# Retention products in two fp32r parts: chunk states and masked scores with v

## Chip, cores and metric

The kernel runs on one core of one Trainium2 chip. The metric is the device time of one launch in microseconds; the median of three runs before the change is 1696.02 us (1693.71 to 1698.85).

## What is computed

A decoder trunk of two residual layers on 1024 positions with 1024 channels, in float32. The even layer has a combined input projection, an S5 state-space branch, a retention branch with four heads, and one output projection; the odd layer is a gated MLP. The change touches the retention branch alone:

```python
    scores = jnp.einsum('bcnhk,bcmhk->bchnm', qc, kc) * decay[None, None]
    inner = jnp.einsum('bchnm,bcmhv->bcnhv', scores, vc)
    local = jnp.einsum('bcmhk,bcmhv->bchkv', kc * zeta[None, None, :, :, None], vc)

    def step(state, s_chunk):
        return state * chunk_decay[None, :, None, None] + s_chunk, state
    ...
    cross = jnp.einsum('bcnhk,bchkv->bcnhv', qc * xi[None, None, :, :, None], prev)
    o = (inner + cross).reshape(bsz, seq, RET_HEADS, RET_DV)
```

Positions are cut into eight chunks of 128. Within a chunk the masked scores multiply v (`inner`); to that comes q times the state that the earlier chunks left (`cross`), and the state grows by k^T v of each chunk (`local`). A group norm per head follows, then a gain and a gate. In the kernel the state update is a plain sum, S + k^T v, and the mask a product with one 128x128 tile, `causal`.

## The kernel before

The work is one long program for one core. TensorE (PE) does the products, VectorE (DVE) and ScalarE (ACT) the elementwise work, GpSimd (POOL) some of it, and SyncE (SP) issues nearly all DMAs, in the order of its queue. Instructions on an engine run in the order in which the program has them; that order comes from a scheduler that sorts by data and buffers, so a change of tiles or buffers moves instructions.

Most products elsewhere take fp32 operands as two fp32r parts: `split` (line 63) casts to hi on ACT and subtracts on DVE to get lo, and `mm3` (line 99) makes three matmuls, hi x hi, hi x lo and lo x hi, summed in PSUM. Retention uses plain fp32 matmuls, each of which stands in the trace as two PE instructions.

`attend(h, nh, ...)` does half of a head's positions, four chunks. There are eight of them, (0,0), (0,1), (1,0) ... (3,1). Its parts: scores k q into `ps_s` (L1100); the mask on DVE, `sd` (L1102); `keys_by_token`, which transposes k into `ps_kt` (L1087) and copies it to `kz` on ACT (L1089); then for each chunk a state product `ps_st` from kz and v (L1112, two of them, and only for seven of a head's eight chunks), a cross product from q and S into `ps_o` (L1115, two), and the inner product from sd and v into the same `ps_o` (L1116); the new state S is the sum of `ps_st` and the old one on DVE (L1122). `ps_o` is copied to `on` by ACT (L1126) and normalised on DVE (L1130 to L1136).

`finish` of that attend is handed to the next one, which calls it between its own key transposes and products (`mid()`). For each of two halves d it loads the gate `bz` (L1143), transposes `on` into `ps_ot` (L1146), makes `yb` = ps_ot x gain x bz on DVE (L1148) and stores it to `yab_d` (L1149). `ps_s`, `ps_kt`, `ps_st` and `ps_ot` are all tiles of the PSUM pool `psE` with the tag "a", and rotate through its three buffers.

The S5 branch's gate, `glu(j)`, fills PE between the steps: `ps_gl` products, a sigmoid `sg` on ACT, products of sg with `yf` and with `az` on DVE (L1073, L1076), and a store of `az` to `yab_d` (L1077).

After the last attend comes the even output projection (`strassen_out`): it loads tiles of `yab_d` (`slB..`, L1226) and weights (`raw`, `wr`, L1238), forms sums of them on DVE (L1274, L1275, L1296, L1297), splits them (`yhi`, `ylo`, `whi`, `wlo`) and multiplies into `ps_acc`. Its tile `t2` (t in the rows, L1274) lies in memory that the retention pools had.

Of the kernel before, what the change touches and what calls it, by code (L numbers as in the profile page):

```python
# [9 lines left out]
F32 = mybir.dt.float32  # L10
F32R = mybir.dt.float32r
# [14 lines left out]
def tile_hybrid_trunk(ctx: ExitStack, tc: tile.TileContext, A, out, dbg=None):  # L26
    nc = tc.nc
    PS = bass.MemoryType.PSUM
    ld = nc.sync.dma_start
# [28 lines left out]
    vv_d = dd("vv_d", [8, 128, 1024])  # L58
# [4 lines left out]
    def split(hi, lo, src, E=nc.vector):  # L63
        nc.scalar.copy(hi, src)  # L64
        E.tensor_tensor(lo, src, hi.bitcast(F32), SUB)  # L65
# [33 lines left out]
    def mm3(ps, lh, ll, rh, rl, first, last, hold=None, chain=False):  # L99
        with tc.issue_after(hold.ins) if hold else ExitStack():  # L100
            nc.tensor.matmul(ps, lh, rh, start=first, stop=False, skip_group_check=chain)  # L101
        nc.tensor.matmul(ps, lh, rl, start=False, stop=False, skip_group_check=chain)  # L102
        return nc.tensor.matmul(ps, ll, rh, start=False, stop=last, skip_group_check=chain)  # L103
# [77 lines left out]
    for e in seqE:  # L181
# [5 lines left out]
        else:  # L187
            nm, h = seqB[e]
# [30 lines left out]
    hh, hl = zip(*[[hp.tile([128, 8, 512], F32R, tag=f"h{e}{t}", name=f"h{e}{t}") for e in "hl"] for t in range(2)])  # L219
# [51 lines left out]
    with tc.tile_pool(name="s5p", bufs=1, reuse_waits="tile") as pp:  # L271
# [234 lines left out]
        for o_, f in zip(ph, (cs, sn)):  # L506
            for k in range(2):
                sl = slice(64 * k, 64 * k + 64)
# [7 lines left out]
        for tabC, tabS, e0, n in ((C0, S0, 0, 16), (C1, S1, 4, 8)):  # L516
            V.memset(tabC[:, :, 0:1], 1.0)
            V.memset(tabS[:, :, 0:1], 0.0)
            m = 1
            while m < n:  # L520
# [4 lines left out]
                cl, sl = tabC[:, :, 0:m], tabS[:, :, 0:m]  # L525
                ch, sh = tabC[:, :, m:2 * m], tabS[:, :, m:2 * m]
# [154 lines left out]
    for n in range(16):  # L681
        b, h = n // 2, n % 2
# [156 lines left out]
    def raw_of(nm, h, t):  # L839
        g, b = {"q": ("q", 4), "k": ("k", 4), "v": ("a2", 2)}[nm]  # L840
        if nm == "v":
            r_ = rq.tile([128, 4, 256], F32, tag=g, name="vraw", bufs=b)
            ld(out=r_, in_=vv_d[4 * t:4 * t + 4, :, h * 256:(h + 1) * 256].rearrange("c p d -> p c d"))
        else:
            r_ = rq.tile([128, 2, 512], F32, tag=g, name=nm + "raw", bufs=b)
            ld(out=r_, in_=qk_d[nm, h][:, :, t * 512:(t + 1) * 512])
        return r_
# [67 lines left out]
    for n, e in enumerate(seqE):  # L915
# [8 lines left out]
        if e == "z":  # L924
            i = cnts["z"]
# [121 lines left out]
    rp = eb.enter_context(tc.tile_pool(name="ret", bufs=1, reuse_waits="tile"))  # L1047
    gy = ExitStack()
    gp = gy.enter_context(tc.tile_pool(name="glu", bufs=1, side="right", reuse_waits="tile"))
# [29 lines left out]
    def keys_by_token(kr, n):  # L1079
        kz = []  # L1080
        for i in range(n):
            if i % 2 == 0:
                m = min(2, n - i)
                pk = psE.tile([128, 2, 2, 128], F32, tag="a", name="ps_kt")
                for c in range(m):
                    for d in range(2):
                        nc.tensor.transpose(pk[:, c, d, :], kr[:, d, (i + c) * 128:(i + c + 1) * 128], ident)  # L1087
                kt = rp.tile([128, 2, 2, 128], F32, tag="kz", name="kz", bufs=3)
                nc.scalar.copy(kt[:, 0:m], pk[:, 0:m])  # L1089
            kz.append(kt[:, i % 2])  # L1090
        return kz

    lastmm = {}

    def attend(h, nh, q, k, v, S, mid=None):
        ps = psE.tile([128, 4, 128], F32, tag="a", name="ps_s")
        for i in range(4):
            c = slice(i * 128, (i + 1) * 128)
            for e in range(2):
                nc.tensor.matmul(ps[:, i, :], k[:, e, c], q[:, e, c], start=e == 0, stop=e == 1)  # L1100
        sd = rp.tile([128, 4, 128], F32, tag="sd", name="sd", bufs=2)
        nc.vector.tensor_tensor(sd, ps, causal.unsqueeze(1).to_broadcast([128, 4, 128]), MUL)  # L1102
        kz = keys_by_token(k, 3 if nh else 4)
        if mid:
            mid()
        po = psO.tile([128, 4, 256], F32, tag="o", name="ps_o")
        for i in range(4):
            c = slice(i * 128, (i + 1) * 128)
            if i < len(kz):
                pl = psE.tile([128, 2, 256], F32, tag="a", name="ps_st")  # L1110
                for d in range(2):
                    nc.tensor.matmul(pl[:, d, :], kz[i][:, d, :], v[:, i, :], start=True, stop=True)  # L1112
            if S is not None:
                for d in range(2):
                    nc.tensor.matmul(po[:, i, :], q[:, d, c], S[:, d, :], start=d == 0, stop=False)  # L1115
            lastmm[h, nh, i] = nc.tensor.matmul(po[:, i, :], sd[:, i, :], v[:, i, :], start=S is None, stop=True)  # L1116
            if i < len(kz):
                Sn = rp.tile([128, 2, 256], F32, tag="S", name="S", bufs=3)
                if S is None:
                    nc.scalar.copy(Sn, pl)  # L1120
                else:
                    nc.vector.tensor_tensor(Sn, pl, S, ADD)  # L1122
                S = Sn
        on = gp.tile([128, 4, 256], F32, tag="on", name="on")
        for e in range(2):
            nc.scalar.copy(on[:, 2 * e:2 * e + 2], po[:, 2 * e:2 * e + 2])  # L1126
        st = small.tile([128, 4, 6], F32, tag="bst", name="bst")
        mv = small.tile([128, 4, 2], F32, tag="bmv", name="bmv")
        for n in range(4):
            nc.vector.bn_stats(st[:, n, :], on[:, n, :])  # L1130
            nc.vector.bn_aggr(mv[:, n, :], st[:, n, :])
        va = small.tile([128, 4], F32, tag="bva", name="bva")
        nc.vector.tensor_scalar(va, mv[:, :, 1], EPS, None, op0=ADD)  # L1133
        r = rstd_of(va, 4)
        for n in range(4):
            nc.vector.tensor_scalar(on[:, n, :], on[:, n, :], mv[:, n, 0:1], r[:, n:n + 1], op0=SUB, op1=MUL)  # L1136
        return (lambda: finish(h, nh, on)), S

    def finish(h, nh, on):
        for d in range(2):  # L1140
            j = 2 * h + d
            bz = gp.tile([128, 512], F32, tag="bz", name="bz", bufs=2)
            ld(out=bz, in_=bz_d[j][:, nh * 512:(nh + 1) * 512])  # L1143
            pt = psE.tile([128, 4, 128], F32, tag="a", name="ps_ot")
            for n in range(4):
                nc.tensor.transpose(pt[:, n, :], on[:, n, d * 128:(d + 1) * 128], ident)  # L1146
            yb = gp.tile([128, 512], F32, tag="yb", name="yb", bufs=2)
            nc.vector.scalar_tensor_tensor(yb, pt.rearrange("p n c -> p (n c)"), cols[:, 8 + j:9 + j], bz, op0=MUL, op1=MUL)  # L1148
            ld(out=yab_d[8 + j][:, nh * 512:(nh + 1) * 512], in_=yb)  # L1149

# [8 lines left out]
    for n, (h, nh) in enumerate(steps):  # L1159
        o = pre[h, nh]  # L1160
        if nh == 0:
            S = None
        if nh == 0:
            pre[h, 1] = prefetch(h, 1)
        e1, S = attend(h, nh, o["q"], o["k"], o["v"], S, e1)
# [235 lines left out]
    gp = odd.enter_context(tc.tile_pool(name="sg", bufs=1, reuse_waits="tile"))  # L1401
# [20 lines left out]
    with tc.tile_pool(name="sv", bufs=2, reuse_waits="tile") as vp, tc.tile_pool(name="psV", bufs=3, space=PS, reuse_waits="tile") as psV, \  # L1422
# [10 lines left out]
        for th in range(2):  # L1433
            acc = [psVa.tile([128, 512], F32, tag="acc", name="ps_v2") for _ in range(4)]
            for u in range(4):
                wu = w_next()
                for kk in range(2):
                    k = 2 * u + kk
                    bh, bl = B[k // 4, th]
                    for i in range(4):  # L1440
                        sl = slice(i * 128, (i + 1) * 128)
# [9 lines left out]
            g = th + 1  # L1451
# [236 lines left out]
```

## Time and profile before

| | |
|---|---|
| runs, us | 1696.02 median (1693.71, 1696.02, 1698.85) |
| profiled execution, us | 1695.32 |
| span of its profile, us | 1693.6 |
| PE busy | 1598.4 us, 94% of the span |
| DVE busy | 1277.3 us, 75% |
| POOL busy | 745.8 us, 44% |
| ACT busy | 609.8 us, 36% |

The profile shows one execution. Times in its rows are microseconds from the start of the span. A busy share over the whole span is an average of stages with different limits, so the tables by stretches of the span say more. In a row of the timeline, [x <-Y] is idle time x of the engine just before the row and what ended it; matmuls overlap, so the time that one costs is read from start to start, and not from its own duration.

### The profile page before, as it was taken

The page shows a single profiled execution, that of the slowest core. Times are in us where ns is not written, and L with a number is a line of the kernel's source. Part 1 is how long each engine was busy: PE and PEld are TensorE (multiplying, and loading weights), DVE is VectorE, ACT ScalarE, POOL GpSimd, SP SyncE. Part 2 cuts the span into 40 slices and gives each one's busy share as a digit, 9 for nine tenths or more (in the row PEclk, how much of TensorE's full clock was granted, in tenths as well). Part 3 has the DMA queues.
Part 4 walks back from the last instruction along what each step waited for, and adds up shares of the span by engine and source line. Part 5 has one row for each costly group of instructions (what it writes and reads, how often), then busy time and mean ns, then how long its engine had stood idle before and what let it go on. Part 6 is the DMA issues. An engine that isn't in the chain of part 4 may idle for free.

```text
span 1693.6 us, 22715 instructions
## 1 busy us (share of the span) xinstructions
PE 1598.4 (94%) x8364; PEld 1351.2 (80%) x8364; DVE 1277.3 (75%) x1951; ACT 609.8 (36%) x787; POOL 745.8 (44%) x521
## 2 busy tenths in 40 slices
PE   7979999998999999999969999899999999989996
PEld 6757888875898977888758888898888888868775
DVE  7857766559778576565896879768988888858876
ACT  6413433432122222122223445332444444442344
POOL 4476876627654432000062544423454444425252
PEclk9989999997999999999989999999999999999998
DMA  8246776641555379654975443434333333388433
GB/s 222 63 124 145 169 184 150 167 128 55 174 181 173 112 265 297 226 192 140 318 276 177 144 155 113 139 106 130 96 103 100 100 100 100 100 291 268 161 125 112
DMA packets 260974, 270.18 MB, mean 160 GB/s; under 512 B 31968, under 2 KB 186368, under 8 KB 260864
## 3 DMA queue, kind: packets, MB, share of 16 engines
q1 hardware_dynamic: 255104, 256.15, 49.6%
q10 hardware_dynamic: 5760, 12.59, 2.0%
q8 instruction: 66, 1.08, 0.3%
q14 instruction: 44, 0.36, 0.1%
HBM read 195.28 MB, written 67.11 MB: 155 GB/s over the span
## 4 chain that ended last, share of the span: by engine, by line
PE 66%; DVE 13%; DMA 9%; issue 5%; POOL 4%; ACT 2%; SPq 1%; POOLq 0%; ACTq 0%; DVEq 0%
PE ps_uz L102 7%; PE ps_uz L103 7%; PE ps_uz L101 7%; PE ps_acc L102 3%; PE ps_vx L102 3%; PE ps_vx L103 3%; PE ps_vx L101 3%; PE ps_acc L101 3%; PE ps_acc L103 3%; DVE wlo L65 3%; PE ps_z L101 2%; PE ps_z L102 2%; PE ps_z L103 2%; PE ps_gl L102 2%; PE ps_gl L103 2%
## 5 line engine op out<-in xcount | busy, mean ns | idle before, releaser
L101 PE MATMUL ps_acc<-whi,yhi 128*128 128x512 f32 x448 | 177.3, 403 | 18.1 <-ACT yhi L64 7.0
L102 PE MATMUL ps_acc<-wlo,yhi 128*128 128x512 f32 x448 | 180.8, 404 | 13.7 <-DVE wlo L65 13.7
L64 ACT CAST whi<-raw 128x1024 fp32r<-128x1024 f32 x110 | 115.6, 1050 | 215.5 <-PE ps_uz L102 49.1
L103 PE MATMUL ps_acc<-whi,ylo 128*128 128x512 f32 x448 | 177.5, 400 | 0.0
L65 DVE TENSOR_TENSOR wlo<-raw,whi 128x1024 fp32r<-128x1024 f32 x94 | 132.2, 1406 | 32.9 <-ACT whi L64 32.1
L101 PEld LDWEIGHTS ps_acc<-whi,yhi 128*128 128x128 f32 x448 | 86.5, 194 | 40.1 <-ACT yhi L64 7.5
L1580 DVE TENSOR_SCALAR vy<-vy,mu,rs 128x128 f32<-128x128 f32 x128 | 113.4, 952 | 2.6 <-DMA vy<-v_d 2.3
L102 PEld LDWEIGHTS ps_acc<-wlo,yhi 128*128 128x128 f32 x448 | 86.8, 194 | 35.7 <-DVE wlo L65 16.4
L103 PEld LDWEIGHTS ps_acc<-whi,ylo 128*128 128x128 f32 x448 | 86.1, 192 | 19.3
L64 ACT CAST whi<-s 128x1024 fp32r<-128x1024 f32 x60 | 62.7, 1047 | 102.3 <-POOL s L724 35.2
L101 PE MATMUL ps_z<-hh,whi 128*128 128x512 f32 (+1 forms) x248 | 95.1, 386 | 0.8 <-ACT hh L64 0.8
L102 PE MATMUL ps_z<-hl,whi 128*128 128x512 f32 (+1 forms) x248 | 95.4, 385 | 0.5 <-DVE hl L65 0.5
L103 PE MATMUL ps_z<-hh,wlo 128*128 128x512 f32 (+1 forms) x248 | 94.0, 379 | 0.0
L65 DVE TENSOR_TENSOR wlo<-s,whi 128x1024 fp32r<-128x1024 f32 x60 | 79.2, 1321 | 16.1 <-ACT whi L64 16.1
L725 POOL TENSOR_TENSOR s<-raw 128x512 f32<-128x512 f32 x25 | 39.0, 1561 | 107.7 <-DMA raw<-in_w_in_odd 83.1
L112 POOL TENSOR_TENSOR rs_r<-bva,nhalf 128x4 f32<-128x4 f32 x8 | 8.5, 1057 | 165.9 <-DVE bva L1133 165.9
L723 POOL TENSOR_TENSOR s<-raw 128x512 f32<-128x512 f32 x25 | 33.7, 1348 | 67.5 <-DMA raw<-in_w_in_odd 28.8
L101 PE MATMUL ps_uz<-hh,whi 128*128 128x512 f32 x144 | 57.3, 398 | 1.1 <-ACT hh L64 0.9
L102 PE MATMUL ps_uz<-hl,whi 128*128 128x512 f32 x144 | 57.1, 396 | 0.0
L103 PE MATMUL ps_uz<-hh,wlo 128*128 128x512 f32 x144 | 56.7, 394 | 0.0
L65 POOL TENSOR_TENSOR wlo<-raw,whi 128x1024 fp32r<-128x1024 f32 x16 | 40.9, 2554 | 34.7 <-ACT whi L64 34.7
L65 DVE TENSOR_TENSOR whl<-raw,whl 128x512 fp32r<-128x512 f32 x25 | 30.4, 1215 | 31.2 <-ACT whl L64 31.2
(561 smaller groups left out, 5133.1 us busy)
## 6 DMA issues: line engine op xcount, KB each, us to landing
raw<-in_w_in_odd SPq DMA_DIRECT2D x50, 512.0 KB, 3.9
raw<-in_w_in_even SPq DMA_DIRECT2D x48, 512.0 KB, 4.2
raw<-in_w_out_even SPq DMA_DIRECT2D x28, 512.0 KB, 4.5
raw<-in_w_out_odd SPq DMA_DIRECT2D x28, 512.0 KB, 4.3
wr<-in_w_out_even SPq DMA_DIRECT2D x16, 512.0 KB, 6.0
vy<-v_d SPq DMA_DIRECT2D x32, 256.0 KB, 3.0
y_d<-c SPq DMA_DIRECT2D x32, 256.0 KB, 3.1
wr<-in_w_out_odd SPq DMA_DIRECT2D x16, 512.0 KB, 4.9
```

What stands on the lines that cost most here:

```text
L64: nc.scalar.copy(hi, src)
L65: E.tensor_tensor(lo, src, hi.bitcast(F32), SUB)
L101: nc.tensor.matmul(ps, lh, rh, start=first, stop=False, skip_group_check=chain)
L102: nc.tensor.matmul(ps, lh, rl, start=False, stop=False, skip_group_check=chain)
L103: return nc.tensor.matmul(ps, ll, rh, start=False, stop=last, skip_group_check=chain)
L112: nc.gpsimd.tensor_tensor(r, v, nhalf[:, 0:n], ALU.pow)
L723: P.tensor_tensor(s14[:, 0:4], a21, a22, ADD)
L725: P.tensor_tensor(s23[:, 4:8], a11, a21, SUB)
L1580: V.tensor_scalar(vy[:, c, :], vy[:, c, :], mu2[:, cc:cc + 1], rs2[:, cc:cc + 1], op0=SUB, op1=MUL)
```

## The change

The state products and the inner products take hi and lo parts of their operands and go through `mm3`: three fp32r matmuls in place of one plain one. For that v is split at the start of each attend (`vh` in a new tile, lo in place of the loaded v, which keeps the name `vraw`), the masked scores into `sh` and `sl`, and the transposed keys, as they leave PSUM, into `kzh` and `kzl`. Cross products and scores stay as they are. To make room, buffers are cut: `sd` 2 to 1, `S` 3 to 2, `bz` 2 to 1, `yb` 2 to 1; `kz` with three becomes two each of `kzh` and `kzl`.

```diff
-            r_ = rq.tile([128, 4, 256], F32, tag=g, name="vraw", bufs=b)
+            r_ = rq.tile([128, 4, 256], F32R, tag=g, name="vraw", bufs=b)
...
-                kt = rp.tile([128, 2, 2, 128], F32, tag="kz", name="kz", bufs=3)
-                nc.scalar.copy(kt[:, 0:m], pk[:, 0:m])
-            kz.append(kt[:, i % 2])
+                kt = [rp.tile([128, 2, 2, 128], F32R, tag="kz" + e, name="kz" + e, bufs=2) for e in "hl"]
+                split(kt[0][:, 0:m], kt[1][:, 0:m], pk[:, 0:m])
+            kz.append([x[:, i % 2] for x in kt])
...
     def attend(h, nh, q, k, v, S, mid=None):
+        vh, vl = rq.tile([128, 4, 256], F32R, tag="x", name="vh", bufs=2), v
+        split(vh, vl, vl.bitcast(F32))
...
-        sd = rp.tile([128, 4, 128], F32, tag="sd", name="sd", bufs=2)
+        sd = rp.tile([128, 4, 128], F32, tag="sd", name="sd")
         nc.vector.tensor_tensor(sd, ps, causal.unsqueeze(1).to_broadcast([128, 4, 128]), MUL)
+        sh, sl = [rp.tile([128, 4, 128], F32R, tag="s" + e, name="s" + e, bufs=1 + (e == "h")) for e in "hl"]
+        split(sh, sl, sd)
...
-                    nc.tensor.matmul(pl[:, d, :], kz[i][:, d, :], v[:, i, :], start=True, stop=True)
+                    mm3(pl[:, d, :], kz[i][0][:, d, :], kz[i][1][:, d, :], vh[:, i, :], vl[:, i, :], True, True)
...
-            lastmm[h, nh, i] = nc.tensor.matmul(po[:, i, :], sd[:, i, :], v[:, i, :], start=S is None, stop=True)
+            lastmm[h, nh, i] = mm3(po[:, i, :], sh[:, i, :], sl[:, i, :], vh[:, i, :], vl[:, i, :], S is None, True)
             if i < len(kz):
-                Sn = rp.tile([128, 2, 256], F32, tag="S", name="S", bufs=3)
+                Sn = rp.tile([128, 2, 256], F32, tag="S", name="S", bufs=2)
...
-            bz = gp.tile([128, 512], F32, tag="bz", name="bz", bufs=2)
+            bz = gp.tile([128, 512], F32, tag="bz", name="bz")
...
-            yb = gp.tile([128, 512], F32, tag="yb", name="yb", bufs=2)
+            yb = gp.tile([128, 512], F32, tag="yb", name="yb")
```

The change also moves instructions, in the retention steps and in the hand-over to the output projection. Line numbers of the changed kernel are four higher there (L1148 becomes L1152, L1274 becomes L1278).

First place: the seventh finish, during the last attend, on DVE. `yb` is the finish's product, `S` the state sum, `az` and `sg` belong to the last gate. Before:

```order
898 L1136 TENSOR_SCALAR on<-on,bmv,rs_r 128x256 x4
899 L1073 TENSOR_TENSOR sg<-sg,yf 128x512
900 L1148 SCALAR_TENSOR_TENSOR yb<-ps_ot,cols,bz 128x512
901 L1076 TENSOR_TENSOR az<-az,sg 128x4x128
902 L1148 SCALAR_TENSOR_TENSOR yb<-ps_ot,cols,bz 128x512
903 L1122 TENSOR_TENSOR S<-ps_st,S 128x512 x2
904 L65 TENSOR_TENSOR wlo<-raw,whi 128x1024
905 L1073 TENSOR_TENSOR sg<-sg,yf 128x512
906 L1122 TENSOR_TENSOR S<-ps_st,S 128x512
```

The same place in the changed kernel, on DVE:

```order
941 L1073 TENSOR_TENSOR sg<-sg,yf 128x512
942 L1076 TENSOR_TENSOR az<-az,sg 128x4x128
943 L1152 SCALAR_TENSOR_TENSOR yb<-ps_ot,cols,bz 128x512
944 L1126 TENSOR_TENSOR S<-ps_st,S 128x512
945 L1152 SCALAR_TENSOR_TENSOR yb<-ps_ot,cols,bz 128x512
946 L1126 TENSOR_TENSOR S<-ps_st,S 128x512
947 L65 TENSOR_TENSOR wlo<-raw,whi 128x1024
948 L1073 TENSOR_TENSOR sg<-sg,yf 128x512
949 L1126 TENSOR_TENSOR S<-ps_st,S 128x512
```

Both `yb` stood ahead of all three S sums; now the second stands behind the first sum and ahead of the other two.

The queue of SP at the same place, with the finish's stores (`yab_d<-yb`), its loads of `bz`, and the first loads of the output projection (`slB10l`). Before:

```order
304 L1149 DMA yab_d_153<-yb 128x512
305 L1143 DMA bz<-bz_d_111 128x512
306 L1149 DMA yab_d_154<-yb 128x512
307 L1143 DMA bz<-bz_d_112 128x512
308 L1226 DMA slB10l<-yab_d_143 128x512
309 L1226 DMA slB10l<-yab_d_144 128x512
310 L1226 DMA slB10l<-yab_d_147 128x512
311 L1226 DMA slB10l<-yab_d_148 128x512
```

And in the changed kernel, on SP:

```order
304 L1153 DMA yab_d_153<-yb 128x512
305 L1147 DMA bz<-bz_d_112 128x512
306 L1230 DMA slB10l<-yab_d_143 128x512
307 L1230 DMA slB10l<-yab_d_144 128x512
308 L1230 DMA slB10l<-yab_d_147 128x512
309 L1153 DMA yab_d_154<-yb 128x512
310 L1147 DMA bz<-bz_d_111 128x512
311 L1230 DMA slB10l<-yab_d_148 128x512
```

The loads of bz before are those of the next finish (111 and 112 are its two halves); now the load behind the first store is the second half of the same finish, and the second store stands behind three loads of slB10l.

Second place: the eighth finish, after the last attend, on DVE in the hand-over. Before, with the first t2 sum (`t`, L1274) some way behind it:

```order
919 L1296 TENSOR_TENSOR slB10h<-slB00h,slB10h 128x1024
920 L1148 SCALAR_TENSOR_TENSOR yb<-ps_ot,cols,bz 128x512 x2
921 L1297 TENSOR_TENSOR slB00h<-slB11h,slB00h 128x1024
922 L65 TENSOR_TENSOR ylo<-slB01h,yhi 128x1024
923 L65 TENSOR_TENSOR wlo<-raw,whi 128x1024
```

And in the changed kernel, on DVE, around its second `yb`:

```order
976 L1301 TENSOR_TENSOR slB00l<-slB11l,slB00l 128x1024
977 L65 TENSOR_TENSOR ylo<-slB01l,yhi 128x1024
978 L65 TENSOR_TENSOR wlo<-raw,whi 128x1024
979 L1152 SCALAR_TENSOR_TENSOR yb<-ps_ot,cols,bz 128x512
980 L1278 TENSOR_TENSOR t_7867<-slB11h,slB10h 128x1024
981 L65 TENSOR_TENSOR wlo<-raw,whi 128x1024
982 L1279 TENSOR_TENSOR slB01h<-slB01h,t_7867 128x1024
```

The first `yb` stays about where both were (directly ahead of the first sum of L1300); the second has moved behind sixteen DVE instructions, straight ahead of the first t2.

## Rows read from the trace of the kernel before

**Rows 1.** The page's chain that ended last, shares of the span by engine.

```profile
PE 66%; DVE 13%; DMA 9%; issue 5%; POOL 4%; ACT 2%; SPq 1%; POOLq 0%; ACTq 0%; DVEq 0%
```

**Rows 2.** Busy time by stretches: PE, PEld, DVE, ACT, POOL; then clock, DMA share.

```profile
600.00:640.00 40.00, 35.82 (x168) 29.21 (x168) 31.98 (x37) 14.38 (x16) 13.33 (x10) 1.00 0.90 299
...
680.00:720.00 40.00, 40.00 (x208) 34.65 (x207) 21.91 (x49) 7.15 (x11) 2.03 (x2) 1.00 0.68 227
720.00:760.00 40.00, 40.00 (x204) 34.29 (x203) 25.81 (x57) 10.06 (x16) 2.01 (x2) 1.00 0.56 186
760.00:800.00 40.00, 40.00 (x207) 34.47 (x206) 22.57 (x52) 9.38 (x15) 2.01 (x2) 1.00 0.43 142
...
840.00:880.00 40.00, 26.88 (x96) 20.33 (x95) 37.52 (x26) 9.32 (x10) 19.03 (x7) 0.83 0.73 249
```

**Rows 3.** Timeline of PE in a retention step: start, duration, line, tiles, count.

```profile
650.13 0.39 PE L101 MATMUL ps_gl<-yhl,whi 128*128 128x512 f32 x1
650.36 0.59 PE L1116 MATMUL ps_o<-vraw,sd 128*128 128x256 f32 x2
650.79 0.59 PE L1112 MATMUL ps_st<-vraw,kz 128*128 128x256 f32 x2
651.22 1.03 PE L1115 MATMUL ps_o<-S,qraw 128*128 128x256 f32 x4
```

**Rows 4.** Timeline of PE in the v projection; thirteen like rows between them.

```profile
452.38 0.28 PE L101 MATMUL ps_vx<-whi,hh 128*128 128x256 f32 x1
...
453.98 0.28 PE L103 MATMUL ps_vx<-whi,hl 128*128 128x256 f32 x1
```

**Rows 5.** The page's costliest groups: ACT casts of 128x1024 (busy, mean ns).

```profile
L64 ACT CAST whi<-raw 128x1024 fp32r<-128x1024 f32 x110 | 115.6, 1050 | 215.5 <-PE ps_uz L102 49.1
```

**Rows 6.** Timeline of DVE around the seventh finish.

```profile
803.35 0.75 DVE L1148 SCALAR_TENSOR_TENSOR yb<-ps_ot,cols,bz 128x512 f32<-128x512 f32 x1 [1.66 <-PE ps_ot L1146]
...
807.10 0.68 DVE L1122 TENSOR_TENSOR S<-ps_st,S 128x512 f32<-128x512 f32 x1
...
809.00 1.22 DVE L65 TENSOR_TENSOR wlo<-raw,whi 128x1024 fp32r<-128x1024 f32 x1
```

**Rows 7.** Timeline of SP around the seventh finish: the issues of DMAs.

```profile
804.12 0.32 SPq L1149 DMA_DIRECT2D yab_d<-yb  x1
804.50 0.42 SPq L1143 DMA_DIRECT2D bz<-bz_d  x1
...
808.10 1.82 SPq L1226 DMA_DIRECT2D slB10l<-yab_d  x4
```

**Rows 8.** Issue to landing: all bz loads, all yb stores, the load at 804.50.

```profile
L1143 SPq DMA_DIRECT2D bz<-bz_d x16: 422/474/1178, 637.4 to 807.6; - x16
DMA to landing us min/median/max: 3.4/5.0/6.5
DMA to landing us min/median/max: 2.3/4.4/7.0
bz<-bz_d SPq DMA_DIRECT2D x1, 256.0 KB, 3.4
```

**Rows 9.** Timeline of PE: the transposes of the seventh finish.

```profile
802.60 1.03 PE L1146 MATMUL ps_ot<-ident,on 128*128 128x128 f32 x8
803.47 1.03 PE L1112 MATMUL ps_st<-vraw,kz 128*128 128x256 f32 x4
```

**Rows 10.** Timeline of SP: the stores of the eighth finish.

```profile
835.47 0.98 SPq L1149 DMA_DIRECT2D yab_d<-yb  x2
```

**Rows 11.** Timeline of DVE in the hand-over.

```profile
841.70 1.23 DVE L65 TENSOR_TENSOR wlo<-raw,whi 128x1024 fp32r<-128x1024 f32 x1 [0.16 <-ACT whi L64]
...
845.12 1.22 DVE L1274 TENSOR_TENSOR t<-slB11h,slB10h 128x1024 f32<-128x1024 f32 x1
...
852.28 2.30 DVE L65 TENSOR_TENSOR wlo<-raw,whi 128x1024 fp32r<-128x1024 f32 x1 [1.01 <-ACT whi L64]
...
858.95 3.39 DVE L1274 TENSOR_TENSOR t<-slB11l,slB10l 128x1024 f32<-128x1024 f32 x1
```

More of the change, by code (lines that the diff above doesn't have):

```diff
@@ L841, in raw_of @@
         if nm == "v":
-            r_ = rq.tile([128, 4, 256], F32, tag=g, name="vraw", bufs=b)
-            ld(out=r_, in_=vv_d[4 * t:4 * t + 4, :, h * 256:(h + 1) * 256].rearrange("c p d -> p c d"))
+            r_ = rq.tile([128, 4, 256], F32R, tag=g, name="vraw", bufs=b)
+            ld(out=r_.bitcast(F32), in_=vv_d[4 * t:4 * t + 4, :, h * 256:(h + 1) * 256].rearrange("c p d -> p c d"))
         else:
```

## Prediction

> **What bounds the kernel now.** I read the chain that ended last first, and then only the stage that the change touches. Over the whole span the chain is mostly TensorE, with VectorE a distant second [rows 1]. The table by stretches then shows two kinds of stage [rows 2]. In the retention steps PE has no idle time at all: in each of the three stretches from 680 to 800 us it is busy for 40.00 of 40 us at the full granted clock, with DVE busy for little over half. A microsecond of matmul taken out there is a microsecond of the end, as long as nothing else is late. From 840 to 880 us, where retention hands over to the even output projection, it is the other way round: DVE is busy for 37.52 of 40 us, PE for 26.88, at a clock of 0.83. There a microsecond of DVE idle time is a microsecond of the end. The change takes work from PE in the first stage and puts a new wait on DVE in both.
>
> **The products.** A plain fp32 product of 128x256 is two PE instructions. The inner product starts at 650.36 us, the state product behind it at 650.79, the cross product at 651.22 [rows 3]: 0.43 us a product. Three fp32r instructions of the same shape are timed by the v projection: 15 of them from 452.38 to 453.98 us, 14 steps in 1.60 us, 0.114 us each, 0.343 us for hi and lo parts together [rows 4]. So each changed product gives back 0.087 us. There are 56 state products (per head four chunks and then three, two halves each) and 32 inner products: 88 x 0.087 = 7.7 us. Cross products and scores stay. The twelve changed products of the first attend I count at nothing: PE is not full there (35.82 of 40 us [rows 2]), since it waits for DVE's split of the S5 output, and the new splits are queued on DVE beside that. 76 x 0.087 = 6.6 us is left.
>
> **The splits.** Each attend gets one cast of v on ScalarE (128x1024, 1.05 us [rows 5]), one of the masked scores (half as wide), and the copy of the transposed keys becomes a cast of the same size: under 2.1 us for ACT, eight times. VectorE gets the lo part of v (1.22 us, as the wlo at 809.00), of the scores and of the two key tiles (each no larger than the S sum at 807.10, 0.68 us [rows 6]): at most 3.3 us an attend. DVE is idle for 14 to 18 of every 40 us there [rows 2], and an attend lasts some 21 us (bz loads of eight finishes from 637.4 to 807.6 us [rows 8]), so this time covers them and PE never sees them: nothing. If that cover failed, the price would be the 3.3 us in each attend.
>
> **Single buffers: the main cost.** A finish turns one step's output (two halves, d = 0 and 1): four transposes into ps_ot, then yb = ps_ot x gain x bz on DVE, then the store. Both bz tiles are loaded a step ahead now, so the two yb follow each other as the order of DVE has them. With one bz and one yb, the second bz load stands on SP behind the first yb's store, and starts only when the first yb has read bz. The chain is: yb(0) starts when its transposes end, 0.3 us before all eight do; 0.77 us later the store is issued (803.35 to 804.12), another 0.38 later the load (804.50) [rows 6, 7]; the load lands after 3.4 to 6.5 us, median 5.0 [rows 8]; then yb(1) takes 0.7. Most loads go out in pairs now, and singly in the new order; such a load is nearest to the one issued at 804.50, with which no other bz load went and which took 3.4 us [rows 8]. But other loads run beside it in most steps, so I take 4.5 us, between that and the median. From the end of the transposes: -0.3 + 1.15 + 4.5 + 0.7 = 6.05 us until yb(1) is done, and 6.65 with an S sum behind it (4.95 and 5.55 at a landing of 3.4; 7.85 and 8.45 at 6.3).
>
> Who waits: yb(1) stands on DVE ahead of S sums, and ps_ot(1) keeps one of the three PSUM buffers that scores, key transposes and state products rotate through. The order of PE says how much work lies between the transposes and the first matmul that needs either. It is counted in four kinds, in this order: fp32r instructions of 512 columns (0.23 us [rows 3]), fp32r of 256 (0.114 [rows 4]), plain 128x256 products (0.43 [rows 3]), and 128x128 instructions (0.109: eight transposes in 0.87 us [rows 9]).
> - finish 2: 1, 30, 2 and 0 of them, 4.5 us, then scores wait for yb(1): 1.5 us idle [0.4 to 3.3].
> - finish 3: 3, 24, 2, 8 = 5.2, then key transposes and a cross product: 1.4 [0.3 to 3.2].
> - finish 4: 0, 30, 2, 0 = 4.3, scores: 1.8 [0.7 to 3.6].
> - finish 5: 0, 21, 3, 12 = 5.0, key transposes: 1.1 [0 to 2.9].
> - finish 6: 9, 21, 1, 0 = 4.9, a state product: 1.2 [0.1 to 3.0].
> - finish 7: 9, 21, 1, 0 = 4.9, the cross product behind S: 1.8; the next S sum then has a wlo (1.22), a gate product and itself behind it (2.35 us) with 0.8 us of matmuls to cover it: 1.6 more. 3.4 [2.3 to 5.2].
>
> Finish 1 has 10 us of cover: nothing. Sum 10.4 us [3.8 to 21]. In finish 7 SP too is held: the second yb store stands ahead of the fourth slB10l load (in the run of four at 808.10 [rows 7]), and the last az store comes behind. The same sum of chain and cover puts that store 3.6 us later than now, in step with PE, so nothing is added for the hand-over's loads.
>
> **The last finish.** Its two yb stand together on DVE now, and their stores go out at 835.47 [rows 10]; the first t2, whose memory the yb tile held, finds them landed and starts at 845.12 without waiting [rows 11]. In the changed order the second yb stands sixteen instructions later, behind the wlo that runs at 841.70, and t2 comes next, waiting for the store just issued. The store lands after 2.3 to 7.0 us, median 4.4 [rows 8]: DVE stands still for about 4.5 us. Some may come back, since DVE waits 1.01 us at 852.28 anyway [rows 11]: 1.4 us at the least, 7.1 at the most. I take 4.5, because the wlo right behind t2 needs weights that are asked for about when they are now, so that idle time likely stays. Some of the work pushed back would then meet a busy GpSimd: at 858.95 the same t2 operation takes 3.39 us instead of 1.22 [rows 11]; this is in neither end.
>
> **Sum:** -6.6 + 10.4 + 4.5 = +8.3 us. Profiled execution: 1695.32 us, with a span of 1693.6, so 1.7 us lie outside; that run is 0.7 us under the median of 1696.02. 1695.3 + 8.3 = **1703.6 us**. At the short ends of all landings: -6.6 + 3.8 + 1.4 = -1.4 us; at the long ends: -6.6 + 21 + 7.1 = +21.5.
>
> **Rivals.**
> 1. Short landings cancel it: every bz load lands like the one at 804.50 (3.4 us) and the last store like the shortest (2.3 us): -1.4 us, **1694 us**, no change that can be told. For it: with one buffer fewer transfers run at once. Against it: 3.4 us is the shortest of sixteen, and the median is 5.0 [rows 8]. The Trainium skill ("DMA: Bandwidth & Descriptors", section "Anatomy of one DMA", a fit made on GpSimd's queue) gives a fixed 2.0 us plus bytes at 436 GB/s; an estimate from it for these 256 KB is 2.6 us, by which only finish 7 would wait (1.5 us), and t2 for some 2.7, or 1692 to 1693 us. The trace disagrees for bz (no landing under 3.4 us), and agrees for the shortest yb store alone.
> 2. The gain is carried whole: PE keeps full, because other waits than I see (the scheduler's order of S sums) give the chain time, and the idle DVE time at t2 is made up by 880 us. -7.7 us, **1687.6 us**, faster. It decides if yb(1) is done within 4.3 to 5.0 us of the transposes in every finish, that is with landings under about 3 us, or if the chain starts earlier than the order shows. For it: PE at 40.00 of 40. Against it: in before yb(1) has no such chain, so nothing in the trace covers it.
> 3. The landings are long: 6.3 us and 7.0 us, near the longest of now, and PE's pauses come on top of one another: +21.5 us, **1717 us**, slower; 1713 and beyond counts here.
>
> **How the numbers follow.** About 0.3%, 5 us, is what a measurement of this kernel can tell from no change: 1691 to 1701 is "same". Forecast (chain costs more than the matmuls give, 1699 to 1712): 0.52, of which a little lies under 1701. Rival 1: 0.26. Rival 2: 0.16. Rival 3: 0.06. That makes faster 0.17, same 0.32, slower 0.51. The range goes from 1690 (leaving out most of rival 2) to 1713 (leaving out rival 3); the forecast's own is 1699 to 1712.
>
> **What would show it.** Right: changed products at 0.343 us a start; DVE idle in front of the second yb of finishes 2 to 7 with DMA bz as what ended it, some 3 to 5 us each; PE waits of 1 to 2 us on yb or S in every step where now it has none; t2 idle some 4 us behind the DMA of yb. Wrong: PE still 40.00 of 40 from 680 to 800 us (then the cover was larger), DVE waits on ps_st instead of bz, or no wait at t2. It would also be wrong if the casts of v made PE wait for ACT.

## The result, and the profile after

The changed kernel takes 1704.9 us, the median of eight runs (1700.39 to 1709.45), against 1694.6 us for the kernel before in eight runs beside it. The ratio is 1.0058 [1.0038, 1.0078]: slower by about 10 us. The forecast was +8.3 us and 1703.6 us. The profiled execution took 1705.59 us, with a span of 1703.9; 1.7 us lie outside the span, as before.

The table by stretches of the changed kernel, with the same columns as [rows 2]:

```profile
680.00:720.00 40.00, 38.47 (x220) 33.24 (x220) 25.47 (x56) 10.08 (x15) 2.03 (x2) 1.00 0.64 218
720.00:760.00 40.00, 37.14 (x210) 32.16 (x209) 27.04 (x54) 12.31 (x19) 3.52 (x2) 1.00 0.53 172
760.00:800.00 40.00, 39.44 (x235) 34.49 (x234) 28.98 (x59) 12.16 (x19) 1.92 (x1) 1.00 0.57 196
...
840.00:880.00 40.00, 26.54 (x107) 20.80 (x106) 31.93 (x24) 9.70 (x10) 16.53 (x6) 0.91 0.74 253
```

PE was full in the three retention stretches; now it stands idle for 1.53, 2.86 and 0.56 us of them. In the hand-over DVE falls from 37.52 us busy to 31.93. The stretches hold slightly later work than the same ones of before, so they say where idle time came in, not how much the end moved.

The waits of PE from 629 to 900 us (line waited at, releaser: us in total, times, longest), those on yb and on S alone:

```profile
PE ps_acc L101 <- DVE yb L1152: 2.8, 1, 2.8
PE ps_s L1102 <- DVE yb L1152: 2.6, 2, 1.9
PE ps_st L101 <- DVE yb L1152: 1.0, 1, 1.0
PE ps_st L101 <- DVE S L1126: 0.9, 2, 0.5
PE ps_o L1119 <- DVE S L1126: 0.8, 1, 0.8
PE ps_kt L1087 <- DVE S L1126: 0.8, 1, 0.8
```

The first row is in the hand-over, at 850.69 us, where PE stands behind the second yb of the last finish; the others are in the retention steps. The same list of the kernel before has one row of this sort, 0.4 us on S. The waits of DVE over the same time, those on DMAs of the changed buffers:

```profile
DVE yb L1152 <- DMA bz<-bz_d: 13.2, 6, 4.2
...
DVE t L1278 <- DMA yab_d<-yb: 4.4, 1, 4.4
...
DVE slB00l L1301 <- DMA slB11l<-yab_d: 3.2, 1, 3.2
```

None of the three is among the waits of before, which has another one of this sort in the hand-over: 2.9 us for a load of slB00h, at 827.39. From issue to landing, first all sixteen bz loads and then all sixteen yb stores, against 3.4/5.0/6.5 and 2.3/4.4/7.0 in [rows 8]:

```profile
DMA to landing us min/median/max: 2.7/4.6/5.9
...
DMA to landing us min/median/max: 2.0/3.7/6.1
```

PE in the changed kernel, in the step of the fourth finish: one chunk (cross and inner products), then the first of the state products, then the wait of the scores; and two state products of the seventh step:

```profile
740.82 1.03 PE L1119 MATMUL ps_o<-S,qraw 128*128 128x256 f32 x4
...
742.05 0.28 PE L101 MATMUL ps_st<-vh,kzh 128*128 128x256 f32 x1
...
744.80 2.05 PE L1102 MATMUL ps_s<-qraw,kraw 128*128 128x128 f32 x16 [1.88 <-DVE yb L1152]
...
813.88 0.28 PE L101 MATMUL ps_st<-vh,kzh 128*128 128x256 f32 x1
...
814.24 0.28 PE L101 MATMUL ps_st<-vh,kzh 128*128 128x256 f32 x1
...
814.60 1.08 PE L1119 MATMUL ps_o<-S,qraw 128*128 128x256 f32 x4
```

A state product, three instructions, takes 0.36 us from start to start (813.88, 814.24, 814.60), 0.120 an instruction; in before it was 0.43 [rows 3]. At 744.80 nothing could start until yb was done. DVE shows why, in the fourth finish, in the seventh, and in the last with the hand-over behind it:

```profile
737.26 0.75 DVE L1152 SCALAR_TENSOR_TENSOR yb<-ps_ot,cols,bz 128x512 f32<-128x512 f32 x1
...
744.00 0.75 DVE L1152 SCALAR_TENSOR_TENSOR yb<-ps_ot,cols,bz 128x512 f32<-128x512 f32 x1 [4.15 <-DMA bz<-bz_d]
...
809.14 0.75 DVE L1152 SCALAR_TENSOR_TENSOR yb<-ps_ot,cols,bz 128x512 f32<-128x512 f32 x1 [1.46 <-PE ps_ot L1150]
...
813.14 0.75 DVE L1152 SCALAR_TENSOR_TENSOR yb<-ps_ot,cols,bz 128x512 f32<-128x512 f32 x1 [2.38 <-DMA bz<-bz_d]
...
849.80 0.74 DVE L1152 SCALAR_TENSOR_TENSOR yb<-ps_ot,cols,bz 128x512 f32<-128x512 f32 x1
854.92 1.23 DVE L1278 TENSOR_TENSOR t<-slB11h,slB10h 128x1024 f32<-128x1024 f32 x1 [4.38 <-DMA yab_d<-yb]
...
862.71 2.65 DVE L1301 TENSOR_TENSOR slB00l<-slB11l,slB00l 128x1024 f32<-128x1024 f32 x1 [3.15 <-DMA slB11l<-yab_d]
```

The second yb of a finish waits for its bz, and the first t2 of the hand-over (854.92) for the store of the last yb; in before that t2 started at 845.12 with no wait [rows 11]. Behind it comes a second wait, 3.15 us for slB11l. SP, whose rows are issues of DMAs, explains both. Its issues in the seventh finish and in the hand-over:

```profile
809.92 0.32 SPq L1153 DMA_DIRECT2D yab_d<-yb  x1
810.29 0.42 SPq L1147 DMA_DIRECT2D bz<-bz_d  x1
...
850.58 0.32 SPq L1153 DMA_DIRECT2D yab_d<-yb  x1
850.95 5.98 SPq L1242 DMA_DIRECT2D wr<-in_w_out_even  x3
856.98 0.46 SPq L1230 DMA_DIRECT2D slB11l<-yab_d  x1
```

The bz load goes out 0.37 us behind the first yb store, as the single buffer forces it to. The last store goes out at 850.58, where the two stores of [rows 10] went together at 835.47. Behind it on the queue stand three weight loads and then the slB11l that DVE waits for. The chain that ended last runs through these (start, duration, what):

```profile
850.58 4.26 DMA yab_d<-yb
...
855.34 1.59 SPq L1242
...
856.98 5.71 DMA slB11l<-yab_d
```

The order of the queue is only part of it. By the kernel's code the half that this last store writes to `yab_d` is the half that this slB11l load reads, so the load could not have gone before the store landed, at 854.83 us. The second of the weight loads waits for the same landing, and the queue adds 2.15 us to it (854.83 to 856.98).

**Where the time went.** I matched the PE instructions that the kernels have in common and took their delays against the first profile of before. The columns are what a stage adds: retention (first scores to the first ps_acc of the output projection) and hand-over (from there to the middle of the projection, about 974 us). Each row is one execution. A second execution of before differs from the first by 3 us in the hand-over alone, so single differences under some 3 us are not read there; in retention the two differ by 0.6.

| profile | retention, us | hand-over, us |
|---|---|---|
| changed kernel, three executions | +3.3, +1.5, +2.7 | +1.4, +1.8, +2.8 |
| before, second execution | +0.6 | -3.1 |
| b_bz1yb1 | +5.7 | +1.5 |
| b_bz1 | +5.4 | +2.0 |
| b_yb1 | +5.2 | +3.9 |
| b_inpl2 | 0.0 | +5.4 |
| a_inpl2 | +0.7 | +0.9 |
| a_last2 | +3.4 | -4.4 |
| a_combo | -0.2 | -3.8 |
| a_pool | -1.3 | -4.8 |
| a_hihi | -14.7 | +3.0 |

Means of the changed kernel less means of before's two: retention 2.5 - 0.3 = +2.2 us, hand-over 2.0 + 1.55 = +3.5, together 5.7. What comes behind has 1.9 more and the code ahead of retention 0.5, which makes 8.1 us in these profiles; the medians of all runs differ by about 10. Neither of those two parts was changed. Behind, it may not be chance alone: the v products of the odd layer (ps_vx) take 148.1, 148.5 and 149.2 us from first to last start in the changed kernel and 147.0 and 147.3 in before, with the instructions in the same order (146.1 to 147.1 in the experiments on before below, 147.1 to 152.9 in those on the changed kernel). Why isn't shown.

### The profile page after: what moved, and what is told of

Same layout as the page of the kernel before. It is cut to its first block, busy times and chain, and to the rows that moved or that the text cites. A ratio compares the mean times of both kernels' runs of the same rounds, so it can differ in the third digit from the quotient of the medians.

```text
span 1703.9 us, 22956 instructions
## 1 busy us (share of the span) xinstructions
PE 1599.4 (94%) x8452; PEld 1354.3 (79%) x8452; DVE 1299.8 (76%) x1983; ACT 622.2 (37%) x803; POOL 748.8 (44%) x521
## 4 chain that ended last, share of the span: by engine, by line
PE 37%; DVE 11%; DMA 7%; issue 4%; POOL 2%; ACT 1%; SPq 0%; POOLq 0%; DVEq 0%; ACTq 0%
PE ps_uz L102 5%; PE ps_uz L103 5%; PE ps_uz L101 5%; PE ps_acc L102 3%; PE ps_acc L101 3%; PE ps_acc L103 3%; DVE wlo L65 2%; PE ps_vx L102 2%; PE ps_vx L101 2%; PE ps_vx L103 2%; PE ps_sg L1593 1%; DMA raw<-in_w_out_odd 1%; DVE ylo L65 1%; PE ps_o L1119 1%; PE ps_gl L101 1%
```

## Experiments

**Theory:** the matmuls give back some microseconds, and the single bz and yb buffers cost more than that, partly through PE's pauses in the steps and partly through the wait at t2. **Rivals:** the cost comes from elsewhere (the splits, the other buffers that were cut), or the matmuls give nothing. No run has the splits with plain products, or `sd`, `S` and `kz` with their old buffers, so the first rival is tested only by what is left when the chain is gone. Below, "us" is (ratio - 1) x 1696.

### The buffers alone, in the kernel before

b_bz1yb1 takes the kernel before and cuts both buffers; b_bz1 and b_yb1 make one of the two cuts each.

```diff
-            bz = gp.tile([128, 512], F32, tag="bz", name="bz", bufs=2)
+            bz = gp.tile([128, 512], F32, tag="bz", name="bz")
...
-            yb = gp.tile([128, 512], F32, tag="yb", name="yb", bufs=2)
+            yb = gp.tile([128, 512], F32, tag="yb", name="yb")
```

> The kernel before with nothing changed but one buffer each for bz and yb. Theory (the single-buffer chain sets the loss): slower than before by 6 to 16 us, about 11, with DVE waits of 2 to 4 us on the bz load in most finishes and a wait of some 4 us at the first t2. Rival (the splits and the new order on DVE and ACT cost the time, buffers are harmless): within 3 us of before.

> The kernel before with one buffer for bz alone, two for yb. Theory: the load is the longer half of the chain, so most of the loss of both (8 us) is here: 5 to 9 us slower than before. Rival (the store of yb sets the pace, by its wait at t2 above all): under 3 us.

> The kernel before with one buffer for yb alone, two for bz. Theory: the second yb waits for the landing of the first one's store, 2 to 7 us, nearly as long as for a load, and t2 waits for the last store: 4 to 8 us slower. Rival (only bz counts): within 3 us of before.

Measured: both 1.005 [1.0034, 1.0065], +8.5 us; bz alone 1.0055 [1.0034, 1.0076], +9.3; yb alone 1.0058 [1.0041, 1.0075], +9.8. DVE's waits from 625 to 900 us in b_bz1yb1, in b_bz1 and in b_yb1:

```profile
DVE yb L1148 <- DMA bz<-bz_d: 10.3, 7, 3.0
...
DVE t L1274 <- DMA yab_d<-yb: 5.2, 1, 5.2
```

```profile
DVE yb L1148 <- DMA bz<-bz_d: 6.0, 6, 2.7
...
DVE t L1274 <- DMA yab_d<-yb: 4.8, 1, 4.8
```

```profile
DVE yb L1148 <- DMA yab_d<-yb: 7.1, 5, 1.9
...
DVE t L1274 <- DMA yab_d<-yb: 3.7, 1, 3.7
```

With no product changed, the buffers alone make the kernel slower by about as much as the whole change does. Either cut by itself is enough, and each was a little dearer than I had put it (5 to 9 and 4 to 8 us): with one yb the second yb waits for the first store to land, with one bz for its load, and the wait at t2 is there in all three. The two cuts don't add; as I read it, because one second half waits for both at once. So it was right to price them as one chain, and a design that gave back only one of the buffers would likely gain nothing.

### The products without the cut buffers

a_inpl2 is the changed kernel with yb written in place over bz and two such tiles, so the memory is the same. Its control, b_inpl2, does that in the kernel before.

```diff
-            bz = gp.tile([128, 512], F32, tag="bz", name="bz")
+            bz = gp.tile([128, 512], F32, tag="bz", name="bz", bufs=2)
...
-            yb = gp.tile([128, 512], F32, tag="yb", name="yb")
+            yb = bz
```

> The changed kernel, with yb written in place over bz and two such tiles: the same memory as one bz and one yb, but both loads of a finish can be made ahead. Theory: the waits on bz and at t2 go, and the gain of the products shows: 3 to 8 us faster than before, 1687 to 1692 us. Rival (splits cost the time): still 5 us or more slower than before.

> The kernel before with yb written in place over bz, two tiles: the control of the run above. Both theories: within 2 us of before. If it is faster by itself, the gain of the run above is not that of the products.

Measured: a_inpl2 1.0003 [0.9986, 1.002], +0.5 us, where the theory had 3 to 8 us faster; b_inpl2 1.0032 [1.0016, 1.0048], +5.4, where both had at most 2. Without the chain the loss is gone, but no gain shows. And the control is not neutral. SP in b_inpl2, around the seventh finish:

```profile
807.06 3.42 SPq L1149 DMA_DIRECT2D yab_d<-bz  x2
810.58 1.95 SPq L1143 DMA_DIRECT2D bz<-bz_d  x2
812.61 2.83 SPq L1226 DMA_DIRECT2D slB10l<-yab_d  x4
```

The next bz loads must now wait until the stores have read the tiles, and SP runs its queue in order, so the first slB10l goes out at 812.61 where before had it at 808.10 [rows 7]. Of these 4.5 us, 2.9 are there already at the first scores (632.7 against 629.8 us), so the queue explains 1.6. The table puts this kernel's whole loss, +5.4 us, in the hand-over; where the rest of it comes from isn't shown.

Between the two kernels that differ by the products and what belongs to them lie 0.5 - 5.4 = -4.9 us, uncertain by some 4 us either way by the two intervals. This looks like the gain of the products, but the profiles don't bear it out: by the table the difference lies in the hand-over (+0.9 against +5.4), where neither kernel's products differ, and hardly in retention (+0.7 against 0.0; a_inpl2's first attend alone was 2 us longer in this execution than a_combo's, 28.25 us against 26.18). So the pair doesn't show what the products give. That a_inpl2 lies some 9 us under the changed kernel shows what the single buffers cost that one.

### The last half finish alone

a_last2 is the changed kernel with one exception: the second half of the last finish takes its two tiles from the tags of the S5 gate, which are free by then. All other finishes keep single buffers.

```diff
+            last = (h, nh, d) == (3, 1, 1)
-            bz = gp.tile([128, 512], F32, tag="bz", name="bz")
+            bz = gp.tile([128, 512], F32, tag="yf" if last else "bz", name="bz", bufs=1 + last)
...
-            yb = gp.tile([128, 512], F32, tag="yb", name="yb")
+            yb = gp.tile([128, 512], F32, tag="sg" if last else "yb", name="yb", bufs=1 + last)
```

> The changed kernel, but the last half of the last finish takes its bz and yb from the buffers of the gate's yf and sg, which are free by then; the other finishes keep their single buffers. Theory: the t2 wait of 4.4 us goes and 2 to 5 us of it reach the end: 5 to 8 us slower than before instead of 10. Rival (what t2 loses is made up later in the stage anyway): as slow as the changed kernel, 9 to 11 us over before.

Measured: 0.9998 [0.9978, 1.0018], -0.3 us, far below the 5 to 8 us of the theory. One half of one finish holds nearly all of the loss. DVE in its hand-over:

```profile
850.26 1.22 DVE L1279 TENSOR_TENSOR t<-slB11h,slB10h 128x1024 f32<-128x1024 f32 x1
...
856.90 1.57 DVE L1302 TENSOR_TENSOR slB00l<-slB11l,slB00l 128x1024 f32<-128x1024 f32 x1 [1.74 <-DMA slB11l<-yab_d]
```

```profile
840.00:880.00 40.00, 31.86 (x129) 25.37 (x128) 37.62 (x25) 10.72 (x11) 17.30 (x6) 0.87 0.87 297
```

t2 follows without a wait, the wait for slB11l falls from 3.15 to 1.74 us, and in the stretch from 840 to 880 us (the second fence, columns as above) DVE is as busy as before the change and PE busier by 5.3 us than in the changed kernel. The table agrees: retention still +3.4 us, as in the changed kernel, but -4.4 in the hand-over, 6.4 less than the changed kernel's mean of +2.0. By ratios the half is worth some 10 us (1.0058 to 0.9998, whose intervals do not meet), where the wait itself is 4.4. The edit takes away more than that wait: the second yb of the last finish is early again, and with it go PE's wait of 2.8 us behind it and 1.4 us of the wait for slB11l. What makes up the rest isn't shown.

### Both together, and the first attend

a_combo writes in place as a_inpl2 does and gives the last finish tiles from the tag "yf". a_pool adds one thing: in the first attend GpSimd makes the lo part of v, not DVE.

```diff
+            last = (h, nh) == (3, 1)
-            bz = gp.tile([128, 512], F32, tag="bz", name="bz")
+            bz = gp.tile([128, 512], F32, tag="yf" if last else "bz", name="bz", bufs=2)
...
-            yb = gp.tile([128, 512], F32, tag="yb", name="yb")
+            yb = bz
```

```diff
-        split(vh, vl, vl.bitcast(F32))
+        split(vh, vl, vl.bitcast(F32), PL if (h, nh) == (0, 0) else nc.vector)
```

> The changed kernel with yb written over bz in two tiles (as in the run with two in-place tiles), and the last finish in the buffers of the gate's yf, so that its loads wait for no store ahead of the slB loads on SP. Theory (the bz chain, the blocked queue and t2 are the whole loss): 3 to 6 us faster than before, 1690 to 1693 us; retention stage within 1 us of before, first slB10l load no later than before. Rival (the hand-over's loss comes from the order of the DVE work, not from the queue): as the run with two in-place tiles, within 2 us of before.

> As the run with yb over bz and the last finish in the buffers of yf, but the first attend's lo part of v is made on GpSimd and not on DVE, where it stands ahead of the splits of the S5 output that PE waits for. Theory: the first attend comes back to the kernel before, 0 to 3 us faster than that run, 1692 to 1695 us. Rival (DVE loses as much to GpSimd at the same time): the same as that run.

Measured: a_combo 1.0 [0.9982, 1.0018], 0 us, where the theory had 3 to 6 us faster; a_pool 0.9984 [0.9966, 1.0002], -2.7 us, the best form of the idea, but with an interval that still holds 1. So the chain and the hand-over are not the whole loss: with both gone, the 5 us that the products give by their durations (below) don't show. Waits of PE and DVE in a_combo from 625 to 900 us, `bz` being the yb that is written over it:

```profile
PE ps_st L101 <- DVE bz L1153: 2.3, 2, 1.2
PE ps_st L101 <- DVE S L1126: 1.0, 2, 0.5
...
DVE vraw L65 <- ACT vh L64: 10.4, 5, 3.4
```

In the steps PE waits 3.5 us on DVE (0.2 of it once more on S), where before has 0.4; none of it is behind a bz load. DVE in turn stands still for 10.4 us until ACT has cast v. The place where that reaches PE is shown below, under the splits.

For the first attend the thought behind a_pool was this: in before DVE splits the S5 output there and PE waits for it, and in the changed kernel DVE has the lo part of v ahead of that (at 630.59 us, for 2.04 us). PE in the changed kernel, behind it:

```profile
637.53 0.79 PE L102 MATMUL ps_gl<-yh,whi 128*128 128x512 f32 x1 [2.33 <-DVE yh L65]
638.13 0.63 PE L103 MATMUL ps_gl<-yhh,wlo 128*128 128x512 f32 x1
638.55 0.63 PE L101 MATMUL ps_gl<-yhh,whi 128*128 128x512 f32 x1
...
641.80 0.40 PE L103 MATMUL ps_gl<-yhh,wlo 128*128 128x512 f32 x1
642.04 0.39 PE L101 MATMUL ps_gl<-yhh,whi 128*128 128x512 f32 x1
```

The profiles don't show that GpSimd helps. From the first scores to those of the second attend a_pool takes 26.58 us and a_combo 26.18, for the same matmuls; PE's waits for yh sum to 5.4 and 4.0 us. The changed kernel takes 26.17, 26.16 and 26.17 us in its three profiles, before 25.29 and 25.91. So the first attend did get longer by 0.3 to 0.9 us (two gate matmuls that moved into it, some 0.5 us, are part of that), but moving the split did not bring that back, and the 2.7 us between the two ratios, whose intervals overlap, are not shown to come from there.

### Fewer matmuls, same buffers

a_hihi is the changed kernel with its splits and its single buffers, and only the hi x hi matmul of each of the 88 products.

```diff
-                    mm3(pl[:, d, :], kz[i][0][:, d, :], kz[i][1][:, d, :], vh[:, i, :], vl[:, i, :], True, True)
+                    nc.tensor.matmul(pl[:, d, :], kz[i][0][:, d, :], vh[:, i, :], start=True, stop=True)
...
-            lastmm[h, nh, i] = mm3(po[:, i, :], sh[:, i, :], sl[:, i, :], vh[:, i, :], vl[:, i, :], S is None, True)
+            lastmm[h, nh, i] = nc.tensor.matmul(po[:, i, :], sh[:, i, :], vh[:, i, :], start=S is None, stop=True)
```

> The changed kernel with only the hi x hi matmul of each of the 88 triples; the hi x lo and lo x hi parts are left out, so 176 matmuls of 0.12 us, 21 us of PE work, are gone; splits, buffers and all waits stay. Theory (the second yb comes by a chain of fixed length, so PE work taken from in front of it returns as waiting): about half comes back, 8 to 13 us faster than the changed kernel, with longer PE waits on yb or S in the finishes. Rival (PE sets the pace, waits are minor): 18 to 21 us faster.

Measured: 0.9947 [0.9929, 0.9965], -9.0 us, and so about 18.7 us less than the changed kernel (1.0057, the mean of its two ratios, less 0.9947). Removed were 176 matmuls of 0.120 us, 21 us. My theory, by which the pauses behind single buffers would eat half of that as their cover shrinks, failed; the rival's 18 to 21 us came true. DVE's wait for bz, and PE's longest wait on yb:

```profile
DVE yb L1152 <- DMA bz<-bz_d: 6.4, 4, 2.8
```

```profile
PE ps_acc L101 <- DVE yb L1152: 4.7, 1, 4.7
```

The waits for bz have halved, not grown. With other durations the scheduler makes another order (DVE's differs from the changed kernel's in many places), and, as I read it, the cover moves along with it. Cover that is counted in one order is good for that order alone.

### Repeats

> The changed kernel unaltered, for a second profile. Expected by every theory: 8 to 12 us slower than before; retention stage (first scores to last inner product) some 3 us longer, hand-over 1 to 3 us longer. If the 2 to 3 us by which the first profile was late ahead of the scores and in the odd layer come back, they belong to the change; if not, they are differences between executions.

> The changed kernel unaltered, a third profile: retention stage 1.5 to 3.5 us longer than before and hand-over 1 to 2 us longer, as in the first two.

> The kernel before unaltered, for a second profile: first scores, last inner product, hand-over and odd layer within 1 us of the first profile relative to each other, if what differs in the changed kernel's profiles there is the change's; else the difference between executions.

The changed kernel again: 1.0056 [1.0034, 1.0078], and 1704.89 us in one run; before again 1695.24 us. The stages of before did not come within 1 us of its first profile, as I had expected: its hand-over is 3.1 us shorter. The wait at t2 is there in all three profiles of the changed kernel (4.4, 4.5 and 4.4 us), with 3.2 to 3.6 us for slB11l behind it, and the waits for bz sum to 13.2, 12.5 and 12.9 us. These belong to the program; the two or three microseconds by which stages differ between executions don't.

## Why the prediction held, point by point

**What bounds.** Right in both stages. PE at 40.00 of 40 in before meant that its work is passed on to the end: a_hihi passes on 18.7 of 21 us. In the hand-over the chain that ended last runs through DVE's second yb and what waits for its store, and an early second yb there (a_last2) is worth some 10 us.

**The products: -6.6 us; by their durations -5.3.** The size that was off is the duration of an fp32r instruction, taken from the v projection at 0.114 us [rows 4]. Here it is 0.120 in state products, and an inner product with the cross product ahead takes 1.23 us (740.82 to 742.05) where before had 0.86 + 0.43 = 1.29 by [rows 3]. So a changed product costs 0.36 us, not 0.343, and saves 0.07; 76 x 0.07 = 5.3 us. No run shows this gain by itself: a_inpl2 and a_combo, which have it without the chain, are no faster than before.

**The chain: +10.4 us; measured 3.4.** The waits listed above without the one at ps_acc sum to 6.1 us, 0.4 in before. Only three of them stand behind a second yb. By finish, with DVE's wait for bz:

| finish | forecast, us | DVE waits for bz | PE waits behind the second yb | PE's other waits on yb and S |
|---|---|---|---|---|
| 1 | 0 | 0 | 0 | 0.52 (S ahead of its first yb) |
| 2 | 1.5 | 2.36 | 0.69 (yb) | 0.81 (S behind an az product) |
| 3 | 1.4 | 2.19 | 0 | 0 |
| 4 | 1.8 | 4.15 | 1.88 (yb) | 0.98 (first yb) |
| 5 | 1.1 | 0.82 | 0 | 0.36 (S ahead of its first yb) |
| 6 | 1.2 | 1.30 | 0 | 0 |
| 7 | 3.4 | 2.38 | 0.84 (S) | 0 |

Only finish 4 came as worked out; 2 gave half of its term. In 7 the bz load issued at 810.29 let yb start at 813.14, under 3 us later, where I had 4.5: the short landing of rival 1, and the place where most was missed (2.6 of 7.0 us). In 3, 5 and 6 the work between covered the chain. So two signs of being right failed: "some 3 to 5 us" of DVE idle time in each finish (only finish 4 is in it), and PE waits of 1 to 2 us in every step. The stages agree with 3.4: retention of the changed kernel (+2.5 in the mean) less that of the three that write in place (a_inpl2, a_combo, a_pool: +0.7, -0.2, -1.3) is 1.8 to 3.8 us. In the kernel before, the same cuts cost that stage some 5 us (b_bz1yb1, b_bz1, b_yb1 in the table).

On landings the Trainium skill ("DMA: Bandwidth & Descriptors", section "Anatomy of one DMA", a fit made on GpSimd's queue) gives by estimate 2.6 us for these 256 KB. The trace agrees for the fastest bz load (2.7 us) and not for the median (4.6, and 3.7 for the stores).

**The last finish: +4.5 us; the wait measured 4.4.** Place and size were right, and so was the doubt that other work pushed back would cost more. What the step lacked is what else hangs on that store and that yb: I priced the store's landing for t2, but not the slB11l load that reads what it writes. In before that load went out at 844.92; now it goes at 856.98 and DVE waits another 3.15 us. PE too waits behind the second yb, 2.8 us at 850.69. The stage gave +3.5 us in the profiles, and taking away this half's single buffers gave 6.4 in the stage and some 10 by ratios.

**The splits: 0; not nothing.** PE waits nowhere directly for the casts of v, and DVE has idle time left in every retention stretch, as forecast. But I counted only how long a split keeps DVE busy, and not how long DVE stands still for it. The lo part of v needs ACT's cast, and the cast needs the load of v. DVE and PE of the changed kernel, ahead of finish 4 and in it:

```profile
731.12 1.23 DVE L65 TENSOR_TENSOR vraw<-vraw,vh 128x1024 fp32r<-128x1024 f32 x1 [2.33 <-ACT vh L64]
...
738.06 0.39 PE L101 MATMUL ps_st<-vh,kzh 128*128 128x256 f32 x1 [0.98 <-DVE yb L1152]
```

ACT started that cast at 730.03, after 3.03 us of waiting for v's load. Behind the lo part DVE has the normalisation, a wlo and the gate's products without a gap, and only then the first yb, at 737.26, on which PE waits 0.98 us. In the three changed kernels that write in place the first yb makes PE wait 1.1 to 2.3 us. So the sign of being wrong, that the casts of v make PE wait for ACT, came true by way of DVE. The first attend, which I left out on the gain side and counted at nothing on the cost side, took 0.3 to 0.9 us more, though its twelve products give some 0.8 there. What the cut of `S` and `sd` adds isn't shown.

**The sum.** +8.3 us forecast, about +10 measured. In retention the products' -5.3, PE's waits (6.1 us, or some 7 counted from start to start, less 0.4 in before) and the first attend's 0.3 to 0.9 make some 1 to 2 us, as the stage has it (+2.2, where the forecast was 10.4 - 6.6 = 3.8). The hand-over gave +3.5, against 4.5, and the parts ahead and behind, for which the forecast has no term, 2.4 in the profiles. So the mechanism and the main wait were right, but the total came out right partly by luck: the chain was priced 7 us too high, and that made up for the splits, for products that give less, and for what no term covered. Rival 1 was right on two of the landings only (3.26 us in finish 6, 2.73 in finish 7); rival 2 fell with PE's idle time, rival 3 since no bz load took over 5.9 us.

## What to carry to other kernels

Two load-compute-store tiles that were double-buffered turn into a chain through the DMA queue when either loses its second buffer, and here the last turn of the loop cost most, since its store holds memory that the next stage wants and writes data that the next stage reads. Before paying for cheaper matmuls with buffers, look whether only the last turn needs the second one: here one half of one finish decided some 10 us. In pricing a delayed store, count who waits for its memory, who reads what it writes, and what stands behind it on its queue. And price an added elementwise step not by its busy time alone, but by what it waits for, since all that stands behind it on its engine waits too.

## What the runs showed of the hardware

- TensorE's clock fell in the first attend of some executions. In the rows at 638 us ps_gl instructions stand 0.42 us apart, and at 641.80 again 0.24. The table by stretches of the changed kernel gives a granted clock of 0.50 from 637.5 to 640 us, the 1.2 GHz level, after PE had waited 2.33 us. The other two profiles of the changed kernel stay at 1.00 there after waits of like length (2.33 and 2.27 us in the second). a_combo had the low clock for longer (0.50 to 0.70 from 642 to 648 us), and of before the second execution had it (0.50 from 638 to 644 us) and the first not. It cost next to nothing in the changed kernel: the first attend takes 26.17 us with it and 26.16 and 26.17 without, since PE then waits less for DVE's yh (3.9 us in total against 5.2 and 5.1). In before it is 25.91 with and 25.29 without.
- The same fp32r instruction of 256 columns took 0.114 us a start in the v projection and 0.120 in the state products.
